# Keeping weight parts in DRAM, a denser last norm and later second parts in a hybrid decoder layer

## The chip, the cores and the metric

The kernel runs on one core of one Trainium2 chip. The metric is the device time of one execution in microseconds (us), taken as the median of several runs. A profile of one further execution shows every instruction.

## The reference

One layer of a decoder for 2048 prompt tokens and 8 sequences of 8 sample tokens, with a model width of 1024:

- RMSNorm, then one input projection to 8 x 512 columns (queries, keys, values and gates of 4 retention heads, and queries, forget gates, inputs and gates of 4 HGRN2 heads, each 128 wide).
- Both head kinds are gated linear recurrences S_t = diag(g_t) S_{t-1} + k_t v_t, o_t = q_t S_t, computed by chunks. Retention has rotary queries and keys and a fixed decay; HGRN2 has a learned decay per element.
- Per-head RMSNorm and a swish gate, then the output projection and the residual.
- RMSNorm, squared-ReLU MLP of width 4096, residual; and a final RMSNorm over the result.

Outputs are the normed activations of both inputs and the recurrent states of both. Everything is float32.

## The kernel before

**Precision by parts.** TensorE multiplies in the format fp32r. To keep float32 accuracy each operand is split into a first part `hi` (a rounded copy, made on ACT) and a second part `lo` = value - `hi` (made on DVE or POOL). A product is three matmuls: hi x hi, hi x lo, lo x hi.

**Groups.** The 2112 token columns go through the layer in three groups of 576, 768 and 768 columns (the samples are in the first). Tokens lie along the free dimension, features along the 128 partitions. For each group, in order: `mix` (input projection and recurrences, head by head), the output projection, and the MLP. The second and third groups do the MLP with a seven-product block scheme (`PRODUCTS`, `OCTET`), for which the first group makes weight sums and keeps them in DRAM (`plan_sums`). The final norm of a group (`finish_first` for the first, `finish` for the others) is done during the next group's first projections.

**Weights.** They come as blocks of 128 x 1024 (512 KB) in a fixed order, the stream. Blocks 0 to 31 are the input projection, 32 to 39 the output projection; they are used once in each group. `weight` runs two blocks ahead: it loads the raw block (L231, SP's DMA queue), makes `hi` on ACT (L256) and has `lo` made by `second_part` (L271), in the projections on POOL for three blocks of four and on DVE for the fourth. There are three buffers for each part, so `hi` of a block can be written when TensorE has finished with the block three before it.

**Order of the work.** The projection loop (`proj`, L323) counts ticks: one for each step of the contraction and part, 24 in a block. Other work is put on an agenda with `later(ticks, ...)` and enters the program between the matmuls when its tick has come. The framework that builds the program then orders each engine's instructions by their place in the program and by estimated times; the hardware runs each engine's instructions in that order. All slabs of 128 x 768 come from one pool of 46.

**The places that the change touches.**

- The head's blocks in `project` come in the order forget gate, HGRN2 query, retention query, retention key, two value blocks; the evacuations are L604 (a multiplication by the norm factor) and, for rotary, L610 and L611 (halves swapped, ACT), L667 (DVE), L668 (POOL) and L669 (DVE). The value matmuls are L687. Two PSUM tiles are used in turn.
- `mixer` forms the HGRN2 scores. The diagonal ("own" products, L823 on POOL) and the pairs inside four tokens ("quad") are split into parts by `cut` (ACT L330, DVE L331) and summed over partitions by matmuls with ones (L469, L470). L777 is the cumulative sum of the logarithms, L792 and L793 the exponents, L837 a masked copy of scores.
- The output projection is done in two passes: three heads (`residual`), and then the last head, a column block of 128 features at a time with 12 matmuls each. After each column block of the last pass comes an addition (L1133 in the first group, L1292 in the others), and the operand of the MLP is split (L1135 and L1136, or L1303 and L1307).
- The final norm squares the eight blocks (L488, L1586 on ACT), adds the squares (L491, L1588), splits the sum (L463/L464, L1370/L1371), sums over partitions, forms the factor (`last_factor`, L1625 to L1627), multiplies (L1232, L1605) and stores y.

Of the kernel before, what the change touches and what calls it, by code (L numbers as in the profile page):

```python
# [9 lines left out]
F32 = mybir.dt.float32  # L10
# [5 lines left out]
P = 128  # L16
D = 1024
KB = D // P
# [28 lines left out]
W_UQ0 = W_DN0 + N_DN  # L47
W_DQ0 = W_UQ0 + N_UP
NW = W_DQ0 + N_DN

# [147 lines left out]
class Kernel:  # L198
# [43 lines left out]
    def weight(self, i):  # L242
        n = len(self.stream)
        while self.w_next < min(i + 1 + self.ahead, n):
            j = self.w_next
            while self.w_load <= j or j >= self.n_first and self.w_load <= j + 2 and self.w_load < n:
                k, later = self.w_load, self.w_load >= self.n_first
                raw = self.raws[k] = self.wp.tile([P, WT], F32, tag="sum" if later and k % 3 else "raw", name="raw",
                                                  bufs=4 if later and k % 3 else 2)
                e = self.stream[k]  # L250
                self.fetch(raw, self.sums[e[1]] if e[0] == "s" else self.I["w"][e[1]])
                self.w_load += 1
            raw = self.raws.pop(j)
            hi = self.wp.tile([P, WT], F32R, tag="hi", name="hi")
            lo = self.wp.tile([P, WT], F32R, tag="lo", name="lo")
            self.nc.scalar.copy(hi, raw)  # L256
# [16 lines left out]
    def plan_stream(self):  # L273

        self.stream = [("w", j) for j in range(W_UP0)]
        up = [[("w", W_UP0 + 4 * t + i) for i in range(4)] for t in range(NQ)]
        dn = [[("w", W_DN0 + 4 * t + i) for i in range(4)] for t in range(NQ)]
        self.stream += up[0]
        for t in range(NQ):
            self.stream += (up[t + 1] if t < NQ - 1 else []) + dn[t]  # L280
        self.n_first = len(self.stream)

        def entry(name, key, i0, pool):
            return ("s", key + (name,), pool) if name[0] == "S" else ("w", i0 + A_PLACE[name], pool)

        for g in range(1, len(GROUPS)):
            self.stream += [("w", j) for j in range(W_UP0)]
            self.stream += [("w", W_UQ0 + i, i % 2) for i in range(4)]
            for t in range(1, NQ):
                self.stream += [entry(name, ("u", t), W_UQ0 + 4 * t, name in ("A12", "S1", "S4")) for name, _ in PRODUCTS]  # L290
            for o in range(NO):
                for k, (name, *_) in enumerate(LAST_OCTET if o == NO - 1 else OCTET):
                    end = g == len(GROUPS) - 1 and o == NO - 1 and k > 4
                    self.stream += [entry(name, ("d", o, v), W_DQ0 + 4 * (2 * o + v), not end and (2 * k + v) % 5 in (1, 3))
                                    for v in range(2)]

    def next_weight(self):
        i = self.w_use
        self.w_use += 1
        r = self.weight(i)  # L300
        self.wts.pop(i - 4, None)
        return r

# [22 lines left out]
                self.tick()  # L326
        return pj[:, :len(pieces), :T2]

    def cut(self, src, hi, lo, T):
        self.tc.keep_in_program_order(self.nc.scalar.copy(hi[:, :T], src[:, :T]))  # L330
        self.nc.vector.tensor_tensor(out=lo[:, :T], in0=src[:, :T], in1=hi.bitcast(F32)[:, :T], op=ALU.subtract)  # L331

    def v2(self, slab, g):
        return slab[:, :g.T].rearrange("p (h t) -> p h t", h=2)
# [14 lines left out]
    def build(self):  # L349
        nc, tc, I = self.nc, self.tc, self.I  # L350
        with ExitStack() as ctx:
# [13 lines left out]
            self.wts, self.second = {}, {}  # L365
            self.blocks = deque()
            self.plan_stream()

# [389 lines left out]
    def mixer(self, g, p, b, t0):  # L758
# [65 lines left out]

        def own_parts():
            x["own_hi"], x["own_lo"] = self.getr(), self.getr()
            self.cut(x["own"], x["own_hi"], x["own_lo"], T)

        def own(sg):
            seg, m = g.segs[sg], len(g.segs[sg])  # L830
# [56 lines left out]

        def quad_parts():
            x["quad_hi"], x["quad_lo"] = self.getr(), self.getr()
            self.cut(x["quad"], x["quad_hi"], x["quad_lo"], T)  # L890

        def quad(sg):
            seg, m = g.segs[sg], len(g.segs[sg])
# [231 lines left out]
    def out_proj_first(self, g):  # L1125
        nc, T = self.nc, g.T
        part = self.residual(g)
        acts = g.oc[H - 1]
        g.acc, h2 = [part[n] for n in range(KB)], {}
        for n in N_ORDER:  # L1130
            pj = self.proj(g, self.take(2), acts)
            acc, hi, lo = g.acc[n], self.getr(), self.getr()
            nc.vector.tensor_tensor(out=self.v2(acc, g), in0=pj, in1=self.v2(acc, g), op=ALU.add)  # L1133
            wf = self.vec[:, V_FFN + n:V_FFN + n + 1]
            nc.scalar.activation(hi[:, :T], acc[:, :T], AF.Copy, scale=wf)  # L1135
            self.later(4, lambda acc=acc, hi=hi, lo=lo, wf=wf: nc.vector.scalar_tensor_tensor(  # L1136
                out=lo[:, :T], in0=acc[:, :T], scalar=wf, in1=hi.bitcast(F32)[:, :T], op0=ALU.mult, op1=ALU.subtract))
            h2[n] = (hi, lo)
        self.flush()
        g.h2 = [h2[n] for n in range(KB)]  # L1140

    def scale_residual_first(self, g):
# [70 lines left out]
    def finish_first(self, g):  # L1213

        nc, T = self.nc, g.T
        x = {"sum": None}

        def square(n):
            x["sum"] = self.add_square(g, x["sum"], g.acc[n])

        def split():
            x["parts"] = self.halves(g, x["sum"])

        def factor():
            r2, x["t"] = self.get(), self.get()
            nc.scalar.activation(r2[:, :T], g.r[:, :T], AF.Square)
            for (c0, c1), ps in zip(g.pieces, self.both_sums(g, x["parts"])):
                self.last_factor(g, ps, r2[:, c0:c1], x["t"][:, c0:c1], c0, c1)
# [12 lines left out]
        self.later(8 * KB + 10, factor)  # L1241


    def plan_sums(self, first, every):
# [32 lines left out]
    def out_proj(self, g):  # L1277
# [5 lines left out]
        for n in N_ORDER:  # L1283
            m, v, i = n // 4, n // 2 % 2, n % 2
            wf = self.vec[:, V_FFN + n:V_FFN + n + 1]
            pj = self.proj(g, self.take(2), acts)
            for h in range(2):
                name = QUARTER[m, h]
                if i == 0:
                    g.R[v][m, h], g.B[v][name] = self.get(), self.get()  # L1290
                r = self.pair(g, g.R[v][m, h])[:, i]
                nc.vector.tensor_tensor(out=r, in0=pj[:, h], in1=self.v2(part[n], g)[:, h], op=ALU.add)  # L1292
# [285 lines left out]
    def finish(self, g, hs=(0, 1), per=None):  # L1578
# [5 lines left out]
        def square(np_, h):  # L1584
            t = self.get()
            nc.scalar.activation(t[:, :T], g.R[np_ % 2][np_ // 2, h][:, :T], AF.Square)  # L1586
            if h in x:
                nc.gpsimd.tensor_tensor(out=x[h][:, :T], in0=x[h][:, :T], in1=t[:, :T], op=ALU.add)  # L1588
            else:
                x[h] = t  # L1590

        def split(h):
            x["parts", h] = self.pair_parts(g, x[h])

        def factor(h):
            hc = slice(h * T2, (h + 1) * T2)
            r2 = x["t", h] = self.get()
            nc.scalar.activation(r2[:, :T2], g.r[:, hc], AF.Square)
            self.last_factor(g, self.pair_sums(g, x["parts", h]), r2[:, :T2], r2[:, :T2], h * T2, (h + 1) * T2)

        def out(np_, h):
            r = self.pair(g, g.R[np_ % 2][np_ // 2, h])
# [20 lines left out]
    def last_factor(self, g, ps, r2, t, c0, c1):  # L1623
# [110 lines left out]
```

## Time and profile before

| | |
|---|---|
| median of 3 runs | 2627.51 us (2626.79 to 2630.17) |
| profiled execution | 2629.84 us |
| its span, first to last instruction | 2628.0 us |
| mean granted TensorE clock | 0.995 |
| DMA traffic | 365.8 MB, mean 139 GB/s |

In a group's line an operation is named by its line in the kernel, its engine, and the tiles that it writes and reads. A wait is written with the engine and line that ended it. PE is TensorE's matmuls and PEld its weight loads, DVE is VectorE, ACT ScalarE, POOL GpSimd, SP the engine whose queue issues the DMAs. The first group's projections run from 0 to about 370 us, its MLP to 792; the second group ends at about 1701.

### The profile page before, as it was taken

The numbers are of one execution on the slowest core, as the hardware profiler recorded it, in microseconds if no ns is written. First come the engines' busy times: TensorE is split into PE (matmuls) and PEld (weight loads), VectorE is DVE, ScalarE is ACT, GpSimd is POOL, SyncE is SP. The second block draws the span as 40 slices with busy tenths as digits, with TensorE's granted clock in tenths as the row PEclk, the third lists the DMA queues.
The fourth block names the chain that finished last, engine by engine and source line by source line (L and its number), as shares of the span: only waits on it lengthen the run. The fifth ranks groups of instructions, "written<-read, shape, count | busy, mean of one in ns | idle before, by whom it ended". The sixth has DMA issues, their size and how long they took to land. (4 is left out here: it accounts for less than half of the span.)

```text
span 2628.0 us, 41634 instructions
## 1 busy us (share of the span) xinstructions
PE 2570.6 (98%) x16999; PEld 2536.8 (97%) x16999; DVE 1683.9 (64%) x2077; ACT 1234.5 (47%) x1653; POOL 1089.9 (41%) x605
## 2 busy tenths in 40 slices
PE   8999999999999999999999999999999999999997
PEld 8999999999999999999999999989999999999997
DVE  6666776545565466565554988675665665549886
ACT  6555442222244555554543545455555445345443
POOL 6555557444436355431222332463554302223322
PEclk9999999999999999999999999999999999999999
DMA  5233366666752111122556755421111225566552
GB/s 181 81 97 90 121 217 241 232 252 221 266 183 85 57 49 49 53 66 69 166 174 203 261 169 199 145 97 49 46 44 59 70 69 178 179 207 209 175 178 81
DMA packets 125951, 365.81 MB, mean 139 GB/s; under 512 B 12480, under 2 KB 33984, under 8 KB 125760
## 3 DMA queue, kind: packets, MB, share of 16 engines
q1 hardware_dynamic: 125616, 363.13, 41.7%
q8 instruction: 134, 2.20, 0.3%
q14 instruction: 57, 0.47, 0.1%
q10 hardware_dynamic: 144, 0.02, 0.0%
HBM read 293.10 MB, written 69.99 MB: 138 GB/s over the span
## 5 line engine op out<-in xcount | busy, mean ns | idle before, releaser
L271 POOL TENSOR_TENSOR lo<-raw,hi 128x1024 fp32r<-128x1024 f32 x227 | 591.3, 2605 | 1257.6 <-ACT hi L256 1140.6
L323 PE MATMUL pj<-slab,hi 128*128 128x288 f32 (+1 forms) x5120 | 1016.8, 316 | 18.9 <-ACT hi L256 6.3
L323 PEld LDWEIGHTS pj<-slab,hi 128*128 128x128 f32 x5120 | 811.8, 189 | 25.2 <-ACT hi L256 9.3
L256 ACT CAST hi<-raw 128x1024 fp32r<-128x1024 f32 x402 | 422.3, 1052 | 847.1 <-PE pj L323 373.3
L323 PE MATMUL pj<-slab,lo 128*128 128x288 f32 (+1 forms) x2560 | 600.1, 315 | 1.8 <-POOL lo L271 1.7
L1105 PE MATMUL pd<-slab,hi 128*128 128x384 f32 x1792 | 457.2, 335 | 6.7 <-DVE slab L1551 3.1
L323 PEld LDWEIGHTS pj<-slab,lo 128*128 128x128 f32 x2560 | 430.0, 189 | 2.9 <-POOL lo L271 2.0
L1105 PE MATMUL pu<-slab,hi 128*128 128x384 f32 x1600 | 396.2, 334 | 0.0
L1105 PEld LDWEIGHTS pd<-slab,hi 128*128 128x128 f32 x1792 | 324.3, 188 | 8.4 <-DVE slab L1551 3.7
L271 DVE TENSOR_TENSOR lo<-raw,hi 128x1024 fp32r<-128x1024 f32 x175 | 231.6, 1323 | 156.0 <-ACT hi L256 152.7
L1105 PE MATMUL pd<-slab,lo 128*128 128x384 f32 x896 | 300.2, 335 | 0.9 <-POOL lo L271 0.9
L1105 PEld LDWEIGHTS pu<-slab,hi 128*128 128x128 f32 x1600 | 288.2, 188 | 0.0
L1105 PE MATMUL pu<-slab,lo 128*128 128x384 f32 x800 | 256.9, 334 | 0.0
L687 PE MATMUL pjv<-hi,slab 128*128 128x256 f32 x1088 | 211.6, 288 | 3.9 <-DVE slab L667 3.9
L1307 DVE TENSOR_TENSOR slab<-slab 128x768 fp32r<-128x768 f32 x144 | 162.3, 1143 | 41.4 <-ACT slab L1303 29.1
L687 PEld LDWEIGHTS pjv<-hi,slab 128*128 128x128 f32 x1088 | 175.5, 193 | 5.6 <-DVE slab L667 4.3
L1105 PEld LDWEIGHTS pd<-slab,lo 128*128 128x128 f32 x896 | 168.8, 188 | 1.5 <-POOL lo L271 1.5
L1303 ACT CAST slab<-slab 128x768 fp32r<-128x768 f32 x144 | 117.9, 833 | 108.3 <-DVE slab L1314 84.9
L687 PE MATMUL pjv<-lo,slab 128*128 128x256 f32 x544 | 155.0, 285 | 0.0
L1105 PEld LDWEIGHTS pu<-slab,lo 128*128 128x128 f32 x800 | 149.3, 188 | 0.0
L1521 DVE TENSOR_TENSOR slab<-pd,slab 128x768 f32<-128x768 f32 x110 | 104.1, 950 | 40.0 <-PE pd L1105 39.7
L797 ACT ACTIVATE slab<-slab 128x768 f32<-128x768 f32 (+2 forms) x72 | 56.3, 781 | 135.8 <-POOL slab L793 135.7
(197 smaller groups left out, 3405.2 us busy)
## 6 DMA issues: line engine op xcount, KB each, us to landing
raw<-w SPq DMA_DIRECT2D x342, 512.0 KB, 3.9
u<-ld SPq DMA_DIRECT2D x64, 384.0 KB, 4.6
slab<-u SPq DMA_DIRECT2D x64, 384.0 KB, 5.8
ld<-x SPq DMA_DIRECT2D x32, 384.0 KB, 4.6
y<-slab SPq DMA_DIRECT2D x12, 384.0 KB, 2.5
raw<-su1S SPq DMA_DIRECT2D x8, 512.0 KB, 3.7
raw<-su2S SPq DMA_DIRECT2D x8, 512.0 KB, 3.9
raw<-su3S SPq DMA_DIRECT2D x8, 512.0 KB, 4.0
```

The costliest lines, as they stand in the source:

```text
L256: self.nc.scalar.copy(hi, raw)
L271: eng.tensor_tensor(out=lo, in0=self.second.pop(j), in1=hi.bitcast(F32), op=ALU.subtract)
L323: self.nc.tensor.matmul(pj[:, i, :T2], w, a[:, c0:c1], start=j == 0 and q == 0, stop=j == n - 1 and q == 2)
L687: nc.tensor.matmul(pj[:, i * 256:(i + 1) * 256], a[:, s:s + C], ww, start=kb == 0 and q == 0, stop=kb == KB - 1 and q == 2)
L797: nc.scalar.activation(x["dd", w][:, a:T], x["dd", w][:, a:T], AF.Exp)
L1105: self.nc.tensor.matmul(*a, **k)
L1303: self.nc.scalar.copy(hi[:, :g.T], B[name][:, :g.T])
L1307: self.nc.vector.tensor_tensor(out=lo[:, :g.T], in0=B[name][:, :g.T], in1=hi.bitcast(F32)[:, :g.T], op=ALU.subtract)
L1521: nc.vector.tensor_tensor(out=r, in0=ps, in1=r, op=ALU.add)
```

## The change

1. **Projection blocks' parts in DRAM.** In the first group, when block 4 to 39 is taken into use, its `hi` and `lo` are stored to DRAM as well (36 blocks, two stores of 512 KB each). In the second and third groups these blocks become stream entries of kind "p": both parts are loaded by two DMAs straight into the part buffers, and no raw block, cast or subtraction is made for them. Blocks 0 to 3 stay as they were. Raw blocks behind a "p" entry aren't loaded ahead of it.
2. **The last norm.** Squares come every 4 ticks instead of 8, the outputs every 5 instead of 6 or 12, and they begin earlier. The squares are added on DVE instead of POOL. The factor's last multiplication comes 4 ticks behind the rest. The very last half of the last group keeps its own distances (`per`).
3. **Second parts.** In `cut` the `lo` of the own and quad products comes 4 or 3 ticks behind `hi`; in the output projection's last pass `lo` comes at 7 ticks instead of 4 (first group, where the agenda is no longer emptied at the end) and at 8 instead of 6 (others).

```diff
+N_MADE = 4
@@ weight
+            e = self.stream[j]
+            if e[0] == "p":
+                self.wts[j] = tuple(self.wp.tile([P, WT], F32R, tag=tag, name=tag) for tag in ("hi", "lo"))
+                for part, kept in zip(self.wts[j], self.kept[e[1]]):
+                    self.nc.sync.dma_start(part.bitcast(F32), kept)
+                self.w_next += 1
+                self.w_load = max(self.w_load, j + 1)
+                continue
...
+                if self.stream[self.w_load][0] == "p":
+                    break
@@ plan_stream
-            self.stream += [("w", j) for j in range(W_UP0)]
+            self.stream += [("p" if j >= N_MADE else "w", j) for j in range(W_UP0)]
@@ next_weight
+        if N_MADE <= i < W_UP0:
+            self.kept[i] = [self.dp.tile([P, WT], F32, name=f"w{i}{part}") for part in ("hi", "lo")]
+            for part, kept in zip(r, self.kept[i]):
+                self.nc.sync.dma_start(kept, part.bitcast(F32))
@@ cut
-        self.nc.vector.tensor_tensor(out=lo[:, :T], in0=src[:, :T], in1=hi.bitcast(F32)[:, :T], op=ALU.subtract)
+        second = lambda: self.nc.vector.tensor_tensor(out=lo[:, :T], in0=src[:, :T], in1=hi.bitcast(F32)[:, :T], op=ALU.subtract)
+        self.later(lag, second) if lag else second()
@@ mixer
-            self.cut(x["own"], x["own_hi"], x["own_lo"], T)
+            self.cut(x["own"], x["own_hi"], x["own_lo"], T, 4)
...
-            self.cut(x["quad"], x["quad_hi"], x["quad_lo"], T)
+            self.cut(x["quad"], x["quad_hi"], x["quad_lo"], T, 3)
@@ out_proj_first
-            self.later(4, lambda acc=acc, hi=hi, lo=lo, wf=wf: nc.vector.scalar_tensor_tensor(
+            self.later(7, lambda acc=acc, hi=hi, lo=lo, wf=wf: nc.vector.scalar_tensor_tensor(
...
-        self.flush()
@@ finish_first
-            x["sum"] = self.add_square(g, x["sum"], g.acc[n])
+            x["sum"] = self.add_square(g, x["sum"], g.acc[n], nc.vector)
...
-            self.later(8 * n, square, n)
-            self.later(8 * KB + 26 + 6 * n, out, n)
-        self.later(8 * KB, split)
-        self.later(8 * KB + 10, factor)
+            self.later(4 * n, square, n)
+            self.later(4 * KB + 22 + 5 * n, out, n)
+        self.later(4 * KB, split)
+        self.later(4 * KB + 10, factor)
@@ out_proj
-                    self.later(6 + 6 * v + 6 * h, lo)
+                    self.later(8 + 6 * v + 6 * h, lo)
@@ finish
-                nc.gpsimd.tensor_tensor(out=x[h][:, :T], in0=x[h][:, :T], in1=t[:, :T], op=ALU.add)
+                (nc.gpsimd if per else nc.vector).tensor_tensor(out=x[h][:, :T], in0=x[h][:, :T], in1=t[:, :T], op=ALU.add)
...
-        pace, wait, gap, each = (3, 8, 6, 3) if per else (8, 10, 16, 12)
+        pace, wait, gap, each = (3, 8, 6, 3) if per else (4, 8, 10, 5)
@@ last_factor
-        self.nc.vector.tensor_tensor(out=t, in0=t, in1=g.r[:, c0:c1], op=ALU.mult)
+        times = lambda: self.nc.vector.tensor_tensor(out=t, in0=t, in1=g.r[:, c0:c1], op=ALU.mult)
+        self.later(lag, times) if lag else times()
```

`finish_first` and `finish` (without `per`) call `last_factor` with a lag of 4; `finish` also squares `g.r` when the sum is split instead of when the factor is formed.

More of the change, by code (lines that the diff above doesn't have):

```diff
@@ L327, in proj, with cut @@
         return pj[:, :len(pieces), :T2]
-    def cut(self, src, hi, lo, T):
+    def cut(self, src, hi, lo, T, lag=0):
         self.tc.keep_in_program_order(self.nc.scalar.copy(hi[:, :T], src[:, :T]))
-        self.nc.vector.tensor_tensor(out=lo[:, :T], in0=src[:, :T], in1=hi.bitcast(F32)[:, :T], op=ALU.subtract)
+        second = lambda: self.nc.vector.tensor_tensor(out=lo[:, :T], in0=src[:, :T], in1=hi.bitcast(F32)[:, :T], op=ALU.subtract)
+        self.later(lag, second) if lag else second()
     def v2(self, slab, g):
@@ L364, in build @@
             self.ahead = 2
-            self.wts, self.second = {}, {}
+            self.wts, self.second, self.kept = {}, {}, {}
             self.blocks = deque()
@@ L1227, in factor @@
             for (c0, c1), ps in zip(g.pieces, self.both_sums(g, x["parts"])):
-                self.last_factor(g, ps, r2[:, c0:c1], x["t"][:, c0:c1], c0, c1)
+                self.last_factor(g, ps, r2[:, c0:c1], x["t"][:, c0:c1], c0, c1, 4)
         def out(n):
@@ L1593, in split @@
             x["parts", h] = self.pair_parts(g, x[h])
+            x["t", h] = self.get()
+            nc.scalar.activation(x["t", h][:, :T2], g.r[:, h * T2:(h + 1) * T2], AF.Square)
         def factor(h):
[L1596 to L1599, printed above, removed]
+            t = x["t", h][:, :T2]
+            self.last_factor(g, self.pair_sums(g, x["parts", h]), t, t, h * T2, (h + 1) * T2, 0 if per else 4)
         def out(np_, h):
@@ L1621, in outputs, with last_factor @@
         return self.O["y"][:, o:o + KB * g.T].rearrange("p (n h t) -> p n h t", n=KB, h=2)[:, :, h]
-    def last_factor(self, g, ps, r2, t, c0, c1):
+    def last_factor(self, g, ps, r2, t, c0, c1, lag=0):
         self.nc.vector.tensor_tensor(out=r2, in0=ps, in1=r2, op=ALU.mult)
         self.rsqrt(t, r2, r2, self.eps, D)
-        self.nc.vector.tensor_tensor(out=t, in0=t, in1=g.r[:, c0:c1], op=ALU.mult)
+        times = lambda: self.nc.vector.tensor_tensor(out=t, in0=t, in1=g.r[:, c0:c1], op=ALU.mult)
+        self.later(lag, times) if lag else times()
     def last_block(self, g, n, h):
```

## Prediction

> **What bounds the kernel now.** The first part of the profile, the busy times, comes first.
>
> ```profile
> PE 2570.6 (98%) x16999; PEld 2536.8 (97%) x16999; DVE 1683.9 (64%) x2077; ACT 1234.5 (47%) x1653; POOL 1089.9 (41%) x605
> ```
>
> TensorE is the bound. The change takes no matmul away, so work removed from ACT, POOL or DVE pays only where TensorE stood still for it. The list of waits, for TensorE alone, prices those places (us in total, times, longest).
>
> ```profile
> PE mm L470 <- DVE slab L331: 8.8, 9, 2.1
> PE pj L323 <- ACT hi L256: 6.3, 1, 6.3
> PE pj L323 <- DVE slab L1198: 5.1, 3, 2.8
> PE pj L323 <- DVE slab L1292: 4.6, 4, 1.2
> PE pjv L687 <- DVE slab L667: 3.9, 2, 2.4
> PE pd L1105 <- DVE slab L1551: 3.1, 2, 2.1
> PE pj L323 <- DVE slab L1133: 2.8, 3, 1.1
> ...
> PE mm L930 <- DVE AT L837: 0.7, 2, 0.5
> ```
>
> All of TensorE's idle time is 46 us, 6.3 of it the start. The lines within reach of the change are L331 (the second part of the own products), L667 (rotary's evacuation), L837, and the additions L1292 and L1133 at the end of the output projections. Not in reach: the start, L1198, L1521 (2.1) and L1551.
>
> Third, the stretch with the longest reachable stall, early in the third group: windows (length, PE, PEld, DVE, ACT, POOL, granted clock, DMA share, GB/s), then the timeline.
>
> ```profile
> 1744.50:1747.00 2.50, 0.32 (x3) 0.11 (x1) 2.50 (x5) 0.09 (x1) 0.00 (x0) 1.00 0.55 203
> 1747.00:1750.40 3.40, 3.23 (x13) 2.85 (x13) 3.40 (x9) 0.00 (x0) 1.29 (x1) 0.51 0.75 236
> 1750.40:1752.60 2.20, 0.08 (x2) 0.06 (x1) 2.11 (x3) 0.84 (x1) 2.20 (x3) 0.99 0.31 115
> ...
> 1753.90:1757.20 3.30, 3.30 (x17) 3.30 (x17) 3.30 (x5) 1.41 (x3) 3.30 (x4) 0.50 0.00 0
> ```
> ```profile
> 1735.01 11.24 DVE L1605 SCALAR_TENSOR_TENSOR slab<-slab,vec 128x384 f32<-128x384 f32 x11
> ...
> 1737.01 2.47 POOL L271 TENSOR_TENSOR lo<-raw,hi 128x1024 fp32r<-128x1024 f32 x1 [3.85 <-ACT hi L256]
> ...
> 1739.44 2.15 POOL L668 TENSOR_TENSOR slab<-slab,ld 128x768 f32<-128x768 f32 x1
> ...
> 1741.56 2.17 POOL L823 TENSOR_TENSOR slab<-slab 128x768 f32<-128x768 f32 x1
> ...
> 1746.17 0.94 DVE L667 TENSOR_TENSOR slab<-pj,ld 128x768 f32<-128x768 f32 x1
> ...
> 1747.17 0.58 PE L687 MATMUL pjv<-hi,slab 128*128 128x256 f32 x1 [2.35 <-DVE slab L667]
> ```
>
> Eleven output multiplications of the previous group's last norm fill DVE for 11.24 us, L667 waits behind them, and the value matmuls wait for the PSUM bank that L667 empties. One L1605 takes 0.61 us (median of 24), but up to 2.76 beside a POOL instruction: eleven at that pace would be 6 us, so three POOL instructions made 5 us of the burst. Two 3.4 us windows at half clock accompany this stall and the next: 2 x 3.4 / 2 = 3.4 us lost that no idle row counts. The second group has the same pattern (1.5, 1.8 and 0.5 us) at full clock.
>
> **The parts kept in DRAM: what is saved.** In groups 2 and 3, 36 blocks each lose a cast (L256, 1.05 us: 76 us of ACT), and a subtraction, 54 on POOL (L271, 2.41 us: 130 us) and 18 on DVE (1.22 us: 22 us). Nearly all lay under matmuls. What lay on the path: before each head's own products, cast (1.05) and L271 (2.40) stood ahead of L610, L611 and L668, and TensorE then waited 0.7 us. POOL starts L668 at 921.62 only because L271 ends then; its input is ready at 920.80, and 1.05 earlier without the cast: the chain to L331 moves up 1.0 to 1.9 us against a wait of 0.7. Six later heads at 0.69: 4.1 us, of which I take 3.8 (bounds 0 and 4.1).
>
> **What is added.** 72 stores and 72 loads more, 37.7 MB each way, about 0.33 us each on SP's queue. The rows for 512 KB: stores (L1261) land after 2.6/4.1/7.6 us, loads (L231) after 2.8/3.8/7.9, four loads in a row (L1253) after 4.3/6.0/7.5. In the first group a block takes some 9 us, so 1.05 MB per block is 116 GB/s on top of 81 to 126. A full share is 326/0.91 = 358 GB/s here: some +0.33 on shares of 0.27 to 0.41, which fits. At the group's end it doesn't:
>
> ```profile
> 310.00:320.00 10.00, 10.00 (x63) 8.08 (x62) 6.98 (x10) 0.27 (x1) 4.04 (x5) 1.00 0.86 272
> ...
> 350.00:360.00 10.00, 8.95 (x66) 8.47 (x64) 8.88 (x11) 2.96 (x4) 0.00 (x0) 1.00 0.96 331
> ```
>
> Nine blocks' stores, 9.4 MB or 26 us of full DMA, meet some 28 us of free share between 310 and 400. Raw blocks can be late by up to 10 us. The block issued at 343.1 lands at 346.8, is cast at 352.1 and is used at about 369: 5 us of cover before the cast, 14 behind it. The stores also hold the part buffers and so the cast three blocks on, but can go once a part is made, two blocks before use. I charge 1.5 us, bounds 0 and 10; a gain is excluded, as nothing is removed there.
>
> In groups 2 and 3 SP waits at the head of its queue until TensorE frees block j-3; y stores, x loads and raw loads queue behind. The tightest cases are the second value block and the second gate block. Its slot is free 48 matmuls ahead (48 x 0.173 = 8.3 us, from 757 matmuls in a 131.0 us window) plus 12 value matmuls at 0.12 = 1.4: 9.7 us. The pair should take 3.8 + 1.5 (the spacing of consecutive landings, 1.2 to 1.6) = 5.3, at the worst row about 9. So cover of 4.4 us; I charge 1 us, bounds 0 and 28 (below).
>
> **The last norm.** Squares every 4 ticks instead of 8, outputs at 51 to 86 ticks instead of 91 to 175 (in the second group at 54 to 89 instead of 90 to 132). A tick is 8.3/24 = 0.35 us, so the sixteen outputs move from the value stage (begins at tick 96) into the third and fourth projection blocks, where DVE stood idle for 5.6, 2.6 and 1.6 us at a time. They need 16 x 0.53 = 8.5 us in some 12, with perhaps two POOL instructions beside them (L660, L668) at 1.8 extra each, since L271 is gone: full, but not beyond. The squares' additions on DVE cost up to 0.95 us (L491 on DVE) instead of up to 1.9 on POOL, thirteen in both groups; ahead of them lies only L604, with a whole block (8.3 us) of cover.
>
> What I expect back: L667's 3.9 -> 3.5, the first heads' own products 1.8 + 2.1 -> 3.3, L837 and L1371 (0.7 + 0.4) -> 0.7, half clock 3.4 -> 3.2: 10.7 us. Bounds: 14.4 if these and the six heads vanish; 0 if the burst merely lands on another evacuation.
>
> [...]
>
> **Second parts behind the next additions.** In the tail of an output projection TensorE spends 12 x 0.173 = 2.1 us per column block, and DVE two additions (0.55 each) and on average one subtraction (0.96): 2.06. DVE loses its lead whenever a subtraction waits for ACT ahead of an addition. Two ticks later the addition can pass. Of 4.6 us (L1292) I take 2.5, since ACT and the buffers for the next sums hold it too; of 2.8 (L1133, lag 4 to 7, flush removed) 1.8. Bounds 0 and 7.4. The first group's postponed subtractions run under its first up block, whose eighth input is needed 42 x 0.13 = 5.5 us in. The lag of 3 or 4 in the own and quad parts only lets another DVE instruction by: nothing, within 0.7 us.
>
> **The sum.** 3.8 + 10.7 + 2.5 + 1.8 - 1.5 - 1.0 = 16.3 us. The profiled execution took 2629.84 us (span 2628.0 and 1.84 around it): 2613.5 by its own time. It lies 2.3 above the median of 2627.51, so 2611.2 there; I say 2612.
>
> **The rivals.**
> - *Only the relief counts.* Instruction order is set when the program is built, from estimated times, so lags may leave it as it was. Then the tails' 4.3 us and part of the burst stay: about 2618. For it: the burst arose from outputs due 12 ticks apart that ran back to back.
> - *The burst moves.* The outputs fall on the rotary blocks' evacuations, and 10.7 is lost; with it some of the heads' gain: 2624, no change. Against it: the idle DVE stretches named above.
> - *Slower: parts land late.* In place of a cast and a subtraction that follow 3.5 us after TensorE frees a buffer, two transfers follow, behind whatever SP waits for; the longest SP wait in the table is 30 us, a y store waiting for L1605. It decides from 9.7 us after release: 16 pairs (two for each of four heads in two groups), late by 1.75 each, cost 28 us, and 2627.5 - 16 + 28 = 2639.5. Even at 1.0 late the gain is gone. For it: two transfers through three buffers; against it: DMA shares of 0.16 to 0.24 there.
> - *No clock back.* The half-clock windows have another cause: 2615.
>
> **How the numbers follow.** Forecast 0.48, only relief 0.20, no clock 0.04, burst moves 0.10, late parts 0.18. The first three are faster by over 0.2% (5.3 us; about what a measurement of this kernel can tell from none): 0.72. The fourth is the same, 0.10; the fifth slower, 0.18. Range: from 2604 (the bounds of the gains with no charge: 16.3 + 2.5 + 5 saved) to 2636, into the late-parts case; the faster cases alone span 2604 to 2621.
>
> **What would show it.** Right: TensorE's waits on L667 gone, on L331 below 2 us, on L1292 and L1133 halved; no half clock near 1747; 330 casts on ACT instead of 402; L1605 in the third and fourth blocks. Wrong: waits of TensorE on DMA into hi or lo, on a cast between 310 and 420, or new ones behind L604 or L667 at the groups' starts.

## The result and the profile after

The changed kernel takes 2605.43 us (median; 2603.20 to 2606.42), against 2627.15 us for the kernel before in the same session: a ratio of 0.9914 (95% interval 0.9897 to 0.9931), 0.9% faster. Its profiled execution took 2605.96 us with a span of 2604.1 us, which is 23.9 us below the span before; the mean granted clock is 0.997.

The busy times of the changed kernel, from the first part of its page:

```profile
PE 2562.1 (98%) x16999; PEld 2532.6 (97%) x16999; DVE 1660.8 (64%) x2072; ACT 1161.2 (45%) x1581; POOL 932.4 (36%) x538
```

The count of matmuls is the same. ACT lost 73 us and POOL 157 us of work, several times what the kernel gained: most of that work had lain under matmuls. The casts are now 330 instead of 402:

```profile
L269 ACT CAST hi<-raw 128x1024 fp32r<-128x1024 f32 x330 | 347.0, 1051 | 746.9 <-PE pj L340 308.1 <-PE pu L1123 174.7 <-PE pd L1123 95.7
```

Then TensorE's waits after (us in total, times, longest). Lines have moved: L256 is now L269, L271 L284, L323 L340, L331 L348, L469 and L470 L487 and L488, L667 and L668 L685 and L686, L687 L705, L1133 L1151, L1198 L1215, L1292 L1309, L1605 L1622.

```profile
PE pj L340 <- DVE slab L1215: 7.2, 5, 2.8
PE pj L340 <- ACT hi L269: 6.1, 1, 6.1
PE pj L340 <- DVE slab L1151: 2.4, 2, 1.6
PE pd L1123 <- DVE slab L1568: 2.1, 1, 2.1
PE pd L1123 <- DVE slab L1538: 2.1, 1, 2.1
PE mm L488 <- DVE slab L348: 1.7, 2, 1.0
```

The waits on rotary's evacuation (L685, 3.9 us before) and on the additions L1309 (4.6 before) are gone, the one on the own and quad second parts (L348) fell from 8.8 to 1.7 us, and no wait on a DMA into `hi` or `lo` has appeared. The wait on L1151 has hardly moved (2.8 to 2.4, its longest longer than before). Out of reach were the start (6.1), L1568, L1538 and L1215; the last rose from 5.1 to 7.2 us. Of its rise, 1.1 us is new and comes of the change: a wait at 793.5, which "Additions on POOL" below explains. TensorE's idle time as a whole fell from 46.3 to 30.7 us: 15.6 us of the 23.9. Windows at half clock, 3.41 us each, stand five times in the trace before and twice in this one (not counting one at the very end of each); at 1.7 us lost in each, that is 5.1 us more. The remaining 3.2 us fit what idle rows undercount (see "Heads" below).

The stretch that was the longest reachable stall, the start of the third group: windows (length, PE, PEld, DVE, ACT, POOL, granted clock, DMA share, GB/s), then DVE's timeline.

```profile
1715.00:1718.00 3.00, 3.00 (x19) 3.00 (x18) 3.00 (x6) 0.61 (x1) 0.11 (x1) 1.00 0.58 217
1718.00:1721.00 3.00, 3.00 (x19) 3.00 (x18) 3.00 (x7) 0.98 (x2) 1.86 (x1) 1.00 1.00 337
1721.00:1724.00 3.00, 3.00 (x19) 3.00 (x19) 2.80 (x3) 0.00 (x0) 1.52 (x1) 1.00 0.92 229
1724.00:1727.00 3.00, 3.00 (x23) 3.00 (x22) 0.00 (x0) 1.28 (x2) 0.00 (x0) 1.00 1.03 391
```
```profile
1711.20 9.61 DVE L1622 SCALAR_TENSOR_TENSOR slab<-slab,vec 128x384 f32<-128x384 f32 x15
1720.74 0.94 DVE L685 TENSOR_TENSOR slab<-pj,ld 128x768 f32<-128x768 f32 x1
1721.61 1.33 DVE L1622 SCALAR_TENSOR_TENSOR slab<-slab,vec 128x384 f32<-128x384 f32 x1
```

All sixteen outputs still run nearly back to back, but at 0.64 us each instead of 1.02, and the last ends at 1722.9, before the first value matmul (1725.5 by the trace). The first L685 is still late, it stands behind the burst; but it ends at 1721.7, 3.8 us before the values begin. TensorE is busy throughout at a granted clock of 1.00, where the kernel before had two windows at half clock.

Where the 23.9 us came from. The table gives the time from the first matmul of a stage to the first of the next, worked out from the traces: before, and the difference of the changed kernel and of four kernels that each do one part of the change (next section).

| stage | before, us | change | parts only | norm only | lags only | stores only |
|---|---|---|---|---|---|---|
| group 1, projections and heads | 292.29 | +0.54 | +0.45 | +0.49 | +1.13 | +1.56 |
| group 1, output projection, three heads | 53.54 | +1.05 | 0 | 0 | +1.06 | 0 |
| group 1, output projection, last pass | 16.30 | -0.35 | -0.01 | 0 | -0.30 | -0.01 |
| group 1, MLP | 423.25 | +0.80 | +0.08 | +1.96 | -0.21 | -1.85 |
| group 2, start (first blocks and values) | 58.40 | -4.48 | -4.57 | -3.49 | -0.13 | +0.01 |
| group 2, the other heads | 291.56 | -3.22 | -3.22 | 0 | 0 | 0 |
| group 2, last pass | 19.51 | -2.86 | -0.05 | 0 | -2.86 | 0 |
| group 2, MLP | 478.67 | -1.53 | +0.08 | -1.51 | 0 | -1.48 |
| group 3, start | 63.70 | -8.61 | -3.77 | -6.43 | 0 | +0.49 |
| group 3, the other heads | 291.46 | -3.12 | -3.10 | 0 | 0 | +0.25 |
| group 3, last pass | 19.51 | -2.87 | -0.06 | 0 | -2.87 | 0 |
| group 3, second half of the MLP | 253.34 | +0.89 | +0.93 | -0.42 | -0.11 | -0.10 |

The first row and the MLP rows differ between kernels that are equal there, so up to 2 us in them is no effect by itself ("stores only" has -1.85 and -1.48 in the MLP rows; in the first row, all but 0.2 us of every difference arises in the first 23 us). The MLP row of group 2 shows what this chance is: -1.5 in the three traces without a half-clock window near 1665, about 0 in the two that have one, as the kernel before does. One part of the MLP row of group 1 is an effect: the wait of 1.1 to 1.2 us at its end, which "norm only" and the change have and the other three don't. The other rows repeat to 0.1 us, but for group 3's start and heads in "stores only" (+0.49, +0.25). Stages that are left out differ by less than 0.1. The rows that repeat say: the starts gave 13.1 us, the other heads 6.3, the last passes 6.1, and one stage lost 1.05.

### The profile page after: what moved, and what is told of

It is laid out like the page before. It is cut to its first block, busy times and chain, and to the rows that moved or that the text cites. A ratio compares the mean times of both kernels' runs of the same rounds, so it can differ in the third digit from the quotient of the medians.

```text
span 2604.1 us, 41673 instructions
## 1 busy us (share of the span) xinstructions
PE 2562.1 (98%) x16999; PEld 2532.6 (97%) x16999; DVE 1660.8 (64%) x2072; ACT 1161.2 (45%) x1581; POOL 932.4 (36%) x538
## 4 chain that ended last, share of the span: by engine, by line
PE 81%; DVE 4%; POOL 2%; issue 2%; ACT 1%; DMA 0%; DVEq 0%; POOLq 0%; ACTq 0%
PE pj L340 34%; PE pd L1123 16%; PE pu L1123 16%; PE pjv L705 5%; PE mm L1123 2%; PE mm L834 1%; PE po L1015 1%; PE mm L1023 1%; PE po L1017 1%; POOL lo L284 1%; DVE slab L509 1%; PE mm L891 1%; PE mm L488 1%; POOL slab L1178 1%; PE mm L487 1%
## 5 line engine op out<-in xcount | busy, mean ns | idle before, releaser
L340 PE MATMUL pj<-slab,hi 128*128 128x288 f32 (+1 forms) x5120 | 1016.2, 316 | 15.9 <-DVE slab L1215 7.2
L284 POOL TENSOR_TENSOR lo<-raw,hi 128x1024 fp32r<-128x1024 f32 x173 | 461.4, 2667 | 1079.4 <-ACT hi L269 993.8
L340 PEld LDWEIGHTS pj<-slab,hi 128*128 128x128 f32 x5120 | 810.9, 189 | 21.7 <-DVE slab L1215 8.1
L269 ACT CAST hi<-raw 128x1024 fp32r<-128x1024 f32 x330 | 347.0, 1051 | 746.9 <-PE pj L340 308.1
L340 PE MATMUL pj<-slab,lo 128*128 128x288 f32 (+1 forms) x2560 | 598.9, 315 | 1.4 <-POOL lo L284 1.2
L340 PEld LDWEIGHTS pj<-slab,lo 128*128 128x128 f32 x2560 | 429.2, 189 | 2.5 <-POOL lo L284 1.5
L284 DVE TENSOR_TENSOR lo<-raw,hi 128x1024 fp32r<-128x1024 f32 x157 | 208.3, 1327 | 146.2 <-ACT hi L269 142.9
L705 PE MATMUL pjv<-hi,slab 128*128 128x256 f32 x1088 | 208.5, 285 | 0.0
L705 PEld LDWEIGHTS pjv<-hi,slab 128*128 128x128 f32 x1088 | 173.4, 191 | 1.4
L705 PE MATMUL pjv<-lo,slab 128*128 128x256 f32 x544 | 153.8, 283 | 0.0
L1538 DVE TENSOR_TENSOR slab<-pd,slab 128x768 f32<-128x768 f32 x110 | 104.2, 950 | 36.9 <-PE pd L1123 36.8
L1273 DVE TENSOR_TENSOR raw<-raw 128x1024 f32<-128x1024 f32 x60 | 104.8, 1746 | 0.6
```

What stands on the lines that cost most here:

```text
L284: eng.tensor_tensor(out=lo, in0=self.second.pop(j), in1=hi.bitcast(F32), op=ALU.subtract)
L340: self.nc.tensor.matmul(pj[:, i, :T2], w, a[:, c0:c1], start=j == 0 and q == 0, stop=j == n - 1 and q == 2)
L705: nc.tensor.matmul(pj[:, i * 256:(i + 1) * 256], a[:, s:s + C], ww, start=kb == 0 and q == 0, stop=kb == KB - 1 and q == 2)
L1273: self.tc.keep_in_program_order(nc.vector.tensor_tensor(out=x[into], in0=x[a], in1=x[b], op=op))
L1538: nc.vector.tensor_tensor(out=r, in0=ps, in1=r, op=ALU.add)
```

## The experiments

Each kernel was run in five rounds against the kernel before. The kernel before took 2629.93 to 2631.95 us on the chips of these runs, so ratios are what to compare.

**Parts only.** The kernel before with the parts in DRAM and nothing else: the "p" entries, the stores and the loads as in the diff, the last norm and all lags as before.

> The parts kept in DRAM alone (stores in the first group, loads of both parts in the others); norm and second parts as before. Theory (relief and distances share the starts of groups 2 and 3): the six later heads give their 6.3 us, the two starts some 6 of the 13.1 us that the whole change gave there (one of the three POOL instructions beside the burst of outputs is gone), the stores cost 1.4: about 2616. Rival 1 (the relief alone clears the starts): 13 us there as well, about 2609. Rival 2 (the distances alone clear them): nothing there, about 2622.

Measured: 2616.09 us, 0.9948 (0.9936 to 0.9961). That is what was expected (2616). The six later heads gain 3.22 and 3.10 us, what the whole change gains there, and both starts gain too, 8.3 us together where some 6 were expected. The outputs' burst stays in the third group, but TensorE's wait behind it moved from the evacuation to the own products. TensorE's waits between 1690 and 1770 us:

```profile
PE mm L487 <- DVE slab L348: 2.2, 1, 2.2
PE mm L947 <- DVE AT L854: 1.0, 1, 1.0
```

So 3.2 us of stalls remain there when only the POOL instructions are gone from beside the burst.

**Norm only.** The kernel before with the last norm's new distances, the additions on DVE and the factor's lag of 4.

> The last norm's distances and its additions on DVE alone; weights and second parts as before. Theory: some 9 of the 13.1 us at the two starts, nothing at the later heads or the tails: about 2618. Rival 1 (the relief alone clears the starts): at most 2 us, 2625 or more. Rival 2 (the distances alone clear them): all 13 us, about 2614.

Measured: 2620.79 us, 0.9966 (0.9954 to 0.9978). The starts gain 3.49 and 6.43 us, 9.9 together. The two parts overlap in the second group (4.57 and 3.49, together 4.48) and add up in large part in the third (3.77 and 6.43, together 8.61). The additions on DVE do cost something: a wait of 1.2 us just before the second group starts (below).

**Lags only.** The kernel before with all four lags, the agenda no longer emptied at the end of the first group's output projection.

> The later second parts alone (own and quad parts, both output projections). Theory: the tails of the output projection in groups 2 and 3 give 2.9 us each, the first group's tail 0.4, the heads nothing, as the own part's wait comes from the cast and the POOL subtraction ahead of it: about 2621. Rival (the tails were cleared by ACT and POOL being free of the weights, not by the lag): no change, 2627. Rival (the lags clear the heads too): 6 us more, 2615.

Measured: 2624.95 us, 0.9981 (0.9972 to 0.9990). The two last passes gain 2.86 and 2.87 us, all of what the whole change gains there. The first group's last pass gains 0.3, and its pass over three heads loses 1.06, which no theory had expected. TensorE's waits between 290 and 420 us:

```profile
PE pj L323 <- DVE slab L1134: 2.4, 2, 1.6
PE pj L323 <- POOL lo L271: 1.8, 1, 1.8
PE mm L471 <- DVE slab L331: 1.0, 1, 1.0
```

The third line is new: the last quad second part of the first group. DVE and POOL around it, from the changed kernel, where the same wait (0.95 us, before the matmul at 308.44) stands:

```profile
304.32 1.43 DVE L348 TENSOR_TENSOR slab<-slab 128x576 fp32r<-128x576 f32 x2 [2.34 <-ACT slab L347]
305.67 0.81 DVE L644 SCALAR_TENSOR_TENSOR slab<-slab,vec 128x576 f32<-128x576 f32 x1
306.40 1.99 DVE L348 TENSOR_TENSOR slab<-slab 128x576 fp32r<-128x576 f32 x1
```
```profile
306.11 1.66 POOL L983 TENSOR_TENSOR slab<-slab 128x576 f32<-128x576 f32 x1 [3.07 <-ACT slab L981]
```

Three ticks later, the subtraction L348 falls behind a gate multiplication (L644) and then meets a POOL instruction: 1.99 us instead of 0.7.

**Stores only.** The kernel before, which also stores the 36 blocks' parts; nothing reads them.

> The 72 stores of the first group alone; the kept parts are never read, and everything else is as before. Theory: the stores cost the 1.4 us that the whole change loses in the first group up to its MLP (0.5 at the first head, 1.0 in the output projection): about 2628.5, with a wait of TensorE near 308 us. Rival (the stores are free, and that loss comes of the other edits): 2627. Rival (DMA saturates between 310 and 400 us): 5 us or more, 2632.

Measured: 2630.53 us, 1.0004 (0.9995 to 1.0013). The total can't tell a loss of 1.5 us from none, as the interval reaches from 1.3 us faster to 3.4 slower. The stages can: the first row's +1.56 arises before the first store is issued (28.3 us), the rest of that row repeats to 0.2 us, and both output projection rows are the same. So the charge of 1.5 us falls, and so does the theory above: the stores cost nothing that shows. The windows at the end of the first group's projections:

```profile
340.00:350.00 10.00, 10.00 (x78) 10.00 (x77) 5.54 (x7) 4.03 (x6) 4.19 (x2) 1.00 0.96 346
350.00:360.00 10.00, 9.21 (x69) 8.98 (x69) 8.89 (x10) 2.50 (x3) 0.62 (x1) 1.00 1.00 367
```

The DMA engines are full, as forecast, and TensorE does not notice. It was busy 8.95 us of the second window before the change and 9.21 here.

**No score lag.** The changed kernel without the lags of the own and quad parts:

```diff
-            self.cut(x["own"], x["own_hi"], x["own_lo"], T, 4)
+            self.cut(x["own"], x["own_hi"], x["own_lo"], T)
...
-            self.cut(x["quad"], x["quad_hi"], x["quad_lo"], T, 3)
+            self.cut(x["quad"], x["quad_hi"], x["quad_lo"], T)
```

> The changed kernel without the lag of the own and quad parts (the second part follows the first at once, as before). Theory: TensorE's wait of 0.95 us near 308 us in the first group, and with it the 1.05 us that its output projection lost, goes; the heads of groups 2 and 3 stay as fast, as the lag did nothing there alone: about 2604.4. Rival (with the relief the lag does matter at the heads): 4 to 6 us slower, 2610.

Measured: 2606.03 us, 0.9902 (0.9886 to 0.9917), not to be told from the change by its time. By stages it is plain: the first group's pass over three heads gets its 1.05 us back, and no head of the later groups changes by more than 0.03. By all rows that repeat, this lag did nothing but that harm.

**Additions on POOL.** The changed kernel with the squares added on POOL again, at the new distances.

> The changed kernel with the squares of the last norm added on POOL again, at the new distances. Theory (POOL needs 1.9 us for each addition but gets one every 1.4 us, beside two multiplications of its own, so the sum and all outputs come some 5 us later, partly into the value stage): the start of group 3 loses 2 to 4 us, 2607 to 2609. Rival (the engine of the additions makes no difference, the distances do): 2605.4.

Measured: 2606.70 us, 0.9908 (0.9895 to 0.9922): no difference as a whole. The third group's start loses 1.71 us, with one new wait of TensorE there, 1.5 us on L1388 (the split of the sum, which POOL now finishes later); the second group's start loses 0.14. So at the third group's start DVE is the better place by 1.7 us, and most of the norm's gain there lies in its other edits.

Just before the second group's start it is the worse place, and the two effects nearly cancel. The additions run while the first group's MLP still ends, and on DVE three of them come between two of its evacuations (L1215), beside a POOL subtraction. DVE, POOL and TensorE in the changed kernel:

```profile
788.10 0.74 DVE L1215 TENSOR_TENSOR slab<-pj,slab 128x576 f32<-128x576 f32 x1
788.76 4.00 DVE L509 TENSOR_TENSOR slab<-slab 128x576 f32<-128x576 f32 x3
792.68 0.75 DVE L1215 TENSOR_TENSOR slab<-pj,slab 128x576 f32<-128x576 f32 x1
```
```profile
787.51 2.91 POOL L284 TENSOR_TENSOR lo<-raw,hi 128x1024 fp32r<-128x1024 f32 x1
```
```profile
793.49 0.79 PE L340 MATMUL pj<-slab,hi 128*128 128x384 f32 x3 [1.13 <-DVE slab L1215]
```

This wait of 1.1 to 1.2 us stands in all six traces with the additions on DVE and this subtraction on POOL. It is in none of the five with the additions on POOL, and not in "subtractions on DVE" (last below), where the subtraction has moved.

**Loads twice and three times.** The changed kernel with each "p" block's two loads issued two or three times, which makes the pair later without changing what is computed.

```diff
-                for part, kept in zip(self.wts[j], self.kept[e[1]]):
-                    self.nc.sync.dma_start(part.bitcast(F32), kept)
+                for _ in range(2):
+                    for part, kept in zip(self.wts[j], self.kept[e[1]]):
+                        self.nc.sync.dma_start(part.bitcast(F32), kept)
```

> The changed kernel with each kept part loaded twice, one transfer behind the other into the same buffer. A pair is then complete some 9 us after TensorE frees the buffer (two landings of 4.1 us and the spacing of 1.2) instead of 5.3. Theory (the tightest pairs, second value block and second gate block, have 9.7 us of cover): within 2 us of the changed kernel, about 2606. Rival (the cover is shorter, because SP's queue is held for the first landing): 16 pairs late by 1 us or more, 2621 or above.

Measured: 2616.52 us, 0.9946 (0.9933 to 0.9958), by the ratios some 8 us slower than the change: neither the theory (within 2 us) nor the rival (16 late pairs). Against the change the two starts lose 6.5 and 4.1 us and every other stage is within the noise. Half of that loss is idle time of TensorE at the starts (5.4 us), the other half is half clock there (10.2 us of it, which loses 5.1). TensorE waits on block 5, the first head's second value block:

```profile
PE pjv L706 <- DMA hi<-w5hi: 2.9, 2, 2.2
...
PE pjv L706 <- DMA lo<-w5lo: 1.3, 1, 1.3
```

Six y stores of the last norm in the second group, and five in the third, stand ahead of it in SP's queue. By the trace of the change `lo` of block 5 lands only 3.8 and 1.7 us ahead of its use, against 5.7 to 6.3 for the second value blocks of the later heads and 13 to 22 us in the projections' other blocks.

> The changed kernel with each kept part loaded three times in a row. A pair is complete some 13 us after the buffer is free. Theory (cover of 9.7 us at 16 pairs): each is late by about 3.3 us, with half-clock windows at most of them: 16 x 3.3 to 16 x 5 = 53 to 80 us more, 2658 to 2685, with TensorE waiting for DMA into hi or lo. Rival (the cover is longer, since other matmuls lie in between): under 10 us more.

Measured: 2695.78 us, 1.0246 (1.0228 to 1.0264): by the ratios some 87 us slower than the change, more than the 53 to 80 expected.

```profile
PE pjv L706 <- DMA lo<-w13lo: 6.9, 2, 3.9
PE pjv L706 <- DMA hi<-w29hi: 6.6, 2, 4.8
...
PE pjv L706 <- DMA hi<-w21hi: 5.7, 2, 4.0
...
PE pj L341 <- DMA lo<-w38lo: 2.7, 2, 2.4
```

The way to be slower that the late-parts rival named exists, then, at three times the traffic, and has its place: the second value blocks (5, 13, 21, 29) and the last blocks of the output projection. The gate blocks, which the rival also counted, are hardly touched (one wait of 1.2 us, block 15); that this is because the mixer's matmuls lie between their release and their use was not tested. Without the stretch at the very end, TensorE runs at half clock for 75 us in this trace, against 7 in the change's: some 34 us of the loss.

**Cast stays.** The changed kernel, where a "p" block loads its raw block and casts it on ACT as before, and only `lo` comes from DRAM.

> The changed kernel, but for a kept block the raw weights are loaded and cast on ACT again, and only the second part comes from DRAM: the same traffic, 72 casts more, no subtraction. Theory (the subtraction on POOL is what held the own products, by being ahead of L668 and by shutting DVE out): the heads of groups 2 and 3 stay at the changed kernel's pace, its starts too; 2605 to 2607. Rival (the cast ahead of the swapped copies is as much of the cause): 0.5 to 1 us back at each of eight heads, 2609 to 2613.

Measured: 2610.20 us, 0.9922 (0.9908 to 0.9935). By its time this falls into the rival's range, but not for the rival's reason: each of the eight heads loses only 0.2 to 0.3 us against the change, 1.9 us in all, and what else differs lies in the first row and the MLP rows. So of the 0.95 to 1.00 us that a later head gained, some 0.7 goes with the subtraction on POOL and 0.2 to 0.3 with the cast.

**Subtractions on DVE.** The results pointed to a cause that none of the change's parts touches: POOL's subtraction L284 beside a stretch in which DVE evacuates for TensorE. This kernel is "no score lag" with six such subtractions given to DVE, one at the first group's output projection and five around group boundaries:

```diff
             pool = self.stream[j][2] if len(self.stream[j]) > 2 else j % 4 and 3 < j
+            if j == 41 or j - self.n_first in (-5, -2, 1, 141, 143):
+                pool = False
```

> The changed kernel without the lag of the own and quad parts, and with the second parts of six raw blocks made on DVE (1.22 us) instead of POOL (2.4 us): one in the first group's last projection pass, three at the end of its MLP, two at the end of the second group's. Theory (the remaining waits there come of a POOL subtraction that shuts DVE out for its whole length): the wait near 366 us falls from 1.6 to under 0.5, those near 745, 768 and 1660 by 1 us each, and some half-clock windows go: 4 to 7 us faster than without the edit, a ratio to the kernel before of 0.987 to 0.989. Rival (DVE is simply full there, wherever the subtraction is made): no change, 0.990 to 0.992.

Measured: 2595.70 us, 0.9866 (0.9853 to 0.9880), 14.5 us faster than "cast stays" on the same chip and by the ratios some 12.6 us faster than the change ((0.9914 - 0.9866) x 2630): the best of all. Against "no score lag", from which it differs in the six subtractions alone, it is 9.5 us faster by the ratios, more than the 4 to 7 expected; in the traces, two half-clock windows fewer (two against four) are 3.4 us of the difference. DVE at the end of the first group's output projection in "no score lag", with the POOL instruction beside it and the matmul that waits:

```profile
361.85 3.67 DVE L1153 SCALAR_TENSOR_TENSOR slab<-slab,vec 128x576 fp32r<-128x576 f32 x2
...
365.45 0.74 DVE L1150 TENSOR_TENSOR slab<-pj,slab 128x576 f32<-128x576 f32 x1
...
362.07 2.83 POOL L284 TENSOR_TENSOR lo<-raw,hi 128x1024 fp32r<-128x1024 f32 x1 [11.46 <-ACT hi L269]
...
366.24 0.79 PE L340 MATMUL pj<-slab,hi 128*128 128x288 f32 x4 [1.63 <-DVE slab L1150]
```

and the same place with the subtraction on DVE:

```profile
361.36 1.68 DVE L1155 SCALAR_TENSOR_TENSOR slab<-slab,vec 128x576 fp32r<-128x576 f32 x2
362.95 1.22 DVE L286 TENSOR_TENSOR lo<-raw,hi 128x1024 fp32r<-128x1024 f32 x1
364.09 1.41 DVE L1152 TENSOR_TENSOR slab<-pj,slab 128x576 f32<-128x576 f32 x2
...
364.89 0.80 PE L342 MATMUL pj<-slab,hi 128*128 128x288 f32 x4 [0.73 <-DVE slab L1152]
```

Two of DVE's multiplications take 1.68 us instead of 3.67, for 1.22 us of work added: DVE arrives earlier with more to do. The wait fell from 1.63 to 0.73 us, not under the 0.5 expected. The list of TensorE's waits shows the same for the end of the first group's MLP, where L1216 (L1215 in the change) is down from 7.2 us to

```profile
PE pj L342 <- DVE slab L1216: 1.6, 3, 0.7
```

By stages the change's kernel loses to it 7.3 us in the first group's MLP, 1.9 in that group's output projection (1.05 of it the score lag) and 1.7 behind. Half clock has no part in the 7.3: that stage has one such window in each of the two traces, at 767.9 in the change and at 417.8 here. The six moves were made together; what each is worth alone was not measured.

## Why the prediction was right, and where its sum was off

The forecast (faster, 2612) was right in sign and, but for the first group's tail and the squares' additions, in mechanism. It was 6.6 us too high: the profiled execution gained 23.9 us where the sum said 16.3. That it stayed inside the range was in part luck: it lies only 1.4 us above the lower end (2604, which took all gains at their bounds and no charge), and one of the four executions, 2603.20, fell below. Term by term:

- **Heads, 3.8 expected, 6.3 measured** ("parts only": 6.3). The mechanism holds: without the cast and POOL's subtraction ahead of rotary, the chain to the own products is earlier by more than the wait. The size failed in the premise that six waits of 0.69 us bound the gain by 4.1. A wait costs more than its idle row. TensorE in the kernel before:

```profile
1106.50 0.33 PE L469 MATMUL mm<-slab,ones_r 128*128 128x384 f32 x1
1107.56 0.44 PE L470 MATMUL mm<-slab,ones_r 128*128 128x384 f32 x1 [0.72 <-DVE slab L331]
1107.84 0.28 PE L687 MATMUL pjv<-hi,slab 128*128 128x256 f32 x1
```

and in the changed kernel:

```profile
1101.91 0.34 PE L487 MATMUL mm<-slab,ones_r 128*128 128x384 f32 x1
1102.09 0.34 PE L488 MATMUL mm<-slab,ones_r 128*128 128x384 f32 x1
1102.26 0.28 PE L705 MATMUL pjv<-hi,slab 128*128 128x256 f32 x1
```

  The idle time counts from the modelled end of the earlier matmul (0.33 us after its start), but the next one can start after 0.18 us. And the matmul behind the wait held up the one after it: 0.28 us from start to start instead of 0.17. From the first to the third start it took 1.34 us before and 0.35 after: the wait cost 0.99 us, not 0.72, and the later heads became 0.95 to 1.00 us shorter.
- **The starts, 10.7 expected, 13.1 measured.** L667's wait went, the own products' and L837's too, and the half clock near 1747 came back, as forecast. Starts and heads together gave 19.4 us, above the bound of 14.4; that bound doesn't follow from its own rows either (3.9 + 8.1 + 1.1 of waits and 3.4 of half clock make 16.5). "Only the relief counts" falls with "norm only" (9.9 us from the norm's edits alone) and with "lags only", though the relief alone gives 8.3 ("parts only"). The reason given for it, a burst of outputs back to back, came true all the same: fifteen still run together. What the distances moved is the burst's place, from beside the value stage to just ahead of it, and POOL's absence its pace (0.64 us each against 1.02; in "parts only" twelve run at 0.61 or 0.62 each). "The burst moves" falls: TensorE waits for nothing behind L685 or L622.
- **The squares' additions, no cost expected, 1.1 us measured.** The prediction saw only L604 ahead of them, with a block of cover. It missed the last evacuations of the first group's MLP, beside which they also run ("Additions on POOL"). In the table this cost lies in the MLP row of group 1.
- **Tails of the second and third group, 2.5 expected, 5.7 measured.** The mis-sized term: I left 2.1 of the 4.6 us to ACT and the buffers, and all of it went, with a further quarter because the idle rows undercount ("lags only": 2.86 and 2.87).
- **First group's tail, 1.8 expected, 0.35 measured.** Here the mechanism was wrong. The lag took away one of three waits (0.78, 0.83 and 1.15 us before; 0.79 and 1.57 after), but the longest was not a matter of order: beside POOL's L271 two of DVE's second parts take 3.12 us before the change instead of 1.55, and a lag of three ticks does not move POOL. "Subtractions on DVE" cut that wait from 1.63 to 0.73 us.
- **Own and quad lags, nothing within 0.7 expected, 1.05 lost**, in one place ("lags only", "no score lag").
- **Stores, 1.5 charged, 0 measured** ("stores only"). The share of 1.00 was foreseen; that blocks needed 14 us later would be touched by it was not so.
- **Late parts, 1.0 charged, 0 measured.** The rival's cover of 9.7 us was about right for the second value blocks of the later heads: the pair takes some 4.5 us and lands about 6.1 us ahead of use, 10.6 together. It was wrong for the first heads, where the y stores stand ahead in the queue. Doubling the loads costs the later heads nothing and the first heads 6.5 and 4.1 us, tripling costs all of them. The count of 16 pairs was wrong at that load: eight second value blocks, and the last blocks of the output projection instead of the gates.

Summed up, 2.5 + 2.4 + 3.2 - 1.45 - 1.05 + 1.5 + 1.0 = 8.1 us more than forecast from these terms; the first group's start and the MLP rows, in which nothing was forecast, took 0.7 back by chance and the additions' wait (+0.54, +0.80, -1.53 and +0.89). That is all but 0.2 of the 7.6 us between 16.3 and 23.9.

## What to carry to other kernels

Before moving a late instruction on DVE, look at what runs on POOL beside it: where DVE stands between two matmuls, a subtraction of 1.2 us on DVE can be cheaper than one of 2.8 us on POOL beside which DVE's own work takes 2 us longer (here 3.67 us instead of 1.68). Before adding work on DVE, look at what it may run ahead of at the end of the stage before. Price a wait of TensorE from start to start of its matmuls, not by the idle time of the row. And test a transfer's cover by doubling the transfer: it shows at once which blocks are tight (here one of 36, beside the y stores) and that the others have room.

## What the runs showed of the hardware

- **Half clock after short stalls.** Windows of 3.41 us at a granted clock of 0.50 stand five times in the trace before, after stalls of 1.75 to 2.81 us, and twice in the trace of the change, after stalls of 2.01 and 2.12 us; other stalls of such lengths are followed by none (1.76 us at 837.7 before, 2.08 us at 1657.6 in the change). The stall at the end of the first group's MLP lasts 2.81 us in the kernel before and 2.82 in the changed one, and only the first is followed by half clock. In each of the two traces the half-clock windows start whole multiples of 3.41 us apart (at 743.52, 767.41, 1668.53, 1747.04 and 1753.87 before; at 767.91 and 2583.80 in the change). On that grid, before and after:

```profile
740.11:743.52 3.41, 0.64 (x5) 0.40 (x4) 3.41 (x4) 2.21 (x3) 0.78 (x1) 1.00 0.41 108
743.52:746.93 3.41, 3.37 (x14) 3.38 (x15) 3.41 (x5) 0.00 (x0) 0.00 (x0) 0.50 0.98 350
```
```profile
740.61:744.02 3.41, 1.60 (x13) 1.37 (x11) 3.41 (x2) 3.19 (x5) 1.75 (x1) 1.00 0.38 154
744.02:747.43 3.41, 2.40 (x18) 2.40 (x19) 3.41 (x6) 0.00 (x0) 0.00 (x0) 1.00 0.89 269
747.43:750.84 3.41, 3.41 (x27) 3.41 (x27) 3.41 (x6) 2.55 (x4) 0.00 (x0) 1.00 0.92 327
```

  Before, the stall falls into one window, in which TensorE is idle for 81%; in the changed kernel it is split over two, idle for 53% and 30%. From 20 us on and without the very end of the kernel, the two traces have six windows at full clock in which TensorE was idle for 58 to 81%, and all six were followed by half clock; of two that were idle for 51% and 53% the first was; of the others, idle for less than 46%, none was. What decides in between is not shown. The stall began 0.64 us into its window in the one trace and 1.60 us in the other, and here that place went with a loss of 1.7 us more (14 matmuls in the window behind it instead of 27 in a full one); what sets the place was not tested.
- **DVE instructions took longer beside a POOL one**, also where POOL's was the one off the critical path. At 740.02 in the changed kernel one of DVE's multiplications (L526) took 3.15 us beside a POOL L284 of 2.44 us that had begun 0.11 us earlier; at 744.90, with no POOL instruction beside it, the same line took 1.00 us. This explains the first group's tail (two second parts in 3.12 us instead of 1.55) and the end of its MLP better than any order of DVE's own work. It was seen the other way too: at 1719.13 in the changed kernel POOL's L686 began while DVE's outputs (0.60 us each) followed each other every 0.53 us. The three beside its start kept that pace, the last one, at 1721.61, took 1.33 us, and L686 took 3.38 us instead of 1.85 (its median).
- **Full DMA engines cost TensorE nothing here.** Over 10 us at a share of 1.00 and 367 GB/s TensorE was busy for 9.21 us, against 8.95 us in the same window before the change, at a share of 0.96 ("stores only").
